# Expert phase of a two-layer hybrid backbone: pairs of experts in units of 64 slots, half of the sums kept in PSUM

## The chip, the core and the metric

One core of a Trainium2 chip runs the whole program. The metric is device time in microseconds (us), the median of several executions. Engines: PE (TensorE, matmuls), DVE (VectorE), ACT (ScalarE), POOL (GpSimd), and SP, which here only starts transfers. Each engine runs its own instruction list in order and waits for others by semaphores.

## The reference

Two layers over 512 tokens of width 1024. Each layer has a mixer (attention and convolution in layer 0, a gated MLP in layer 1) and then a mixture of experts, the part that the change touches:

```python
def hier_moe(h, ...):                       # 512 tokens, D 1024
    gidx = argmax(group logits)             # one of 4 groups, weight gw
    tv, ti = lax.top_k(expert logits of that group, 2)
    ew = softmax(tv) * gw                   # 2 of 32 experts for a token
    for e in range(32):                     # D_EXPERT 256
        he = (silu(t @ w_gate[e]) * (t @ w_up[e])) @ w_down[e]
        out = out + dense_w[:, e:e + 1] * he
x = x + g2 * hier_moe(h2)
```

512 tokens with two experts each are 1024 slots, 32 for an expert on the mean, but the router decides how many each expert gets.

## The kernel before

The 32 experts are taken as 16 pairs (e, e + 16), and for each pair SP streams six tiles of 1 MB. Tokens are first sorted by expert into four tiles `xs`, so that an expert's tokens are a run of columns. A pair unit takes 64 slots of each of both experts:

- gates and up, `gate_up` (L357): 16 matmuls of 512 columns, the two experts in the two halves of the array's columns, into bank `pg`;
- `act` (L362 on ACT, L363 on DVE) and `turn` (L370 transposes, L371 copy) give the hidden activations, transposed;
- `down` (L430): 8 matmuls into two banks `py`;
- `weigh` (L419 on DVE, L420 on ACT, L421 on DVE): multiplies by the token's weight and by g2 and splits the product in a rounded high part and a rest, so that the scatter can use the faster fp32r matmuls;
- `add_half` (L400): a matmul with a one-hot matrix (L388, L389) brings each of the four token tiles and two column halves back to token order, once for the high part and once for the rest, and DVE (L413) or ACT and POOL (L410, L411) add the half to X.

If an expert of the pair has more than 64 tokens, `again` runs a unit for the next 64 of that expert (L451 gates, L459 down) in another part of PSUM. That is decided at run time by `tc.If`. Both arms of the If (L623) hold the gates of the next pair (`first(j + 1, ...)`), with the scatter of this pair behind them in PE's list; a hint on PE (L480, L482) names the likely arm ahead of time. The order of everything is that of the Python code; there is no scheduler.

In PE's list a pair is thus: `down` of j, branch, gates of j + 1, scatter of j in two parts around the transposes of j + 1, `down` of j + 1. DVE's weighing of j has the time of the gates of j + 1. Weight tiles for the next pairs are asked for at the end of each pair (`st.emit(6, j)`, issued at L322 and L324).

Of the kernel before, what the change touches and what calls it, by code (L numbers as in the profile page):

```python
# [8 lines left out]
F32 = mybir.dt.float32  # L9
# [8 lines left out]
P = 128  # L18
# [3 lines left out]
SLOT = 64  # L22

# [93 lines left out]
class Route:  # L117
# [37 lines left out]
    def end(self, res):  # L155
# [23 lines left out]
        R0 = k.work.tile([P, 8, 64], BF16, name="R0", tag="w2", bufs=NW2)  # L179
# [22 lines left out]
        with nc.allow_low_precision(reason="whole numbers under 512"):  # L202
            v.tensor_reduce(res.g0, p0[:, 0:2], axis=AX.X, op=OP.add)
# [10 lines left out]
        pin(v.tensor_copy(it[:, 0], ro[:, 0]))  # L214
# [8 lines left out]
    def starts(self, res):  # L223

        k, cc = self.k, self.cc
        v = k.nc.vector
        cm = k.small.tile([P, 16], F32, name="cm", tag="cm")
        for r in range(8):
            v.tensor_scalar(res.start[:, r], cc[:, 32:64], float(SLOT * r), 1024.0 - SLOT, op0=OP.add, op1=OP.min)
        v.tensor_tensor(cm, cc[:, 0:16], cc[:, 16:32], op=OP.max)  # L230
        v.tensor_copy(res.cnt[:, 0, :], cm)
        res.most = k.work.tile([P, 1], I32, name="most", tag="most")
        v.tensor_reduce(res.most, cm, axis=AX.X, op=OP.max)
        v.tensor_scalar(cc[:, 0:32], cc[:, 0:32], float(SLOT), None, op0=OP.is_gt)
        v.scalar_tensor_tensor(res.cnt[:, 2, :], cc[:, 16:32], 2.0, cc[:, 0:16], op0=OP.mult, op1=OP.add)
        v.tensor_scalar(cc[:, 0:16], cm, 2.0 * SLOT, None, op0=OP.is_gt)
        v.scalar_tensor_tensor(res.cnt[:, 3, :], res.cnt[:, 2, :], 3.0, cc[:, 0:16], op0=OP.is_equal, op1=OP.max)
        v.tensor_scalar(cm, cm, float(SLOT - 1), None, op0=OP.add)
        v.tensor_copy(res.cnt[:, 1, :], cm)
        v.tensor_scalar(res.cnt[:, 1, :], res.cnt[:, 1, :], 6, None, op0=OP.arith_shift_right)  # L240

        d = k.small.tile([P, 2, 16], F32, name="d", tag="rd")
        v.tensor_scalar(d[:, 0], res.cnt[:, 2, :], 2.0, None, op0=OP.is_equal)
        v.tensor_tensor(d[:, 1], res.start[:, 1, 16:32], res.start[:, 1, 0:16], op=OP.subtract)
        v.tensor_tensor(d[:, 1], d[:, 1], d[:, 0], op=OP.mult)
        v.tensor_tensor(res.second, d[:, 1], res.start[:, 1, 0:16], op=OP.add)
# [27 lines left out]
    def columns(self, r):  # L274
# [8 lines left out]
        for c, C in enumerate(self.C):  # L283
# [3 lines left out]
            v.tensor_tensor(C[:, :, 0], C[:, :, 0], b(k.tok1[:, s]), op=OP.mult)  # L287

# [45 lines left out]
def moe_bufs(k):  # L334
# [15 lines left out]
    return m  # L350


def gate_up(k, m, st, p, cs):

    for c in cs:
        for h in range(2):
            k.nc.tensor.matmul(m.pg[64 * h:64 * h + 64, :], m.xT[:, c, 64 * h:64 * h + 64], st.gu(p, h, c), start=(c == 0), stop=(c == 7))  # L357


def act(k, m):  # L360

    k.nc.scalar.activation(m.sg, m.pg[:, 0:256], AF.Silu)  # L362
    k.nc.vector.tensor_tensor(m.h, m.sg, m.pg[:, 256:512], op=OP.mult)  # L363


def turn(k, m, n=P):

    nc = k.nc
    for f in range(2):
        nc.tensor.transpose(m.ph[:, f * P:f * P + n], m.h[0:n, f * P:(f + 1) * P], k.ident[0:n, 0:n])  # L370
    nc.scalar.copy(m.hT[:, :, 0:n], m.ph[:, 0:2 * P].rearrange("p (f s) -> p f s", f=2)[:, :, 0:n])  # L371


SIDE = [(0, 1), (2, 0)]
SIDE0 = ()


class Outs:
# [3 lines left out]
    def __init__(self, oh, y):  # L382
        self.oh, self.y = oh, y
        self.left = ()

    def where(self, k, m, tok):
        eng = k.nc.vector
        eng.tensor_scalar(m.t4, k.noff, tok, None, op0=OP.add)  # L388
        eng.tensor_tensor(self.oh.rearrange("p (i t) -> p i t", i=NT), k.iota[:, None, :].to_broadcast([P, NT, P]),  # L389
                                m.t4[:, :, None].to_broadcast([P, NT, P]), op=OP.is_equal)  # L390

    def add(self, k, m, X, tiles):

        for i in tiles:
            for n in range(2):
                self.add_half(k, m, X, i, n)

    def sum_half(self, k, po, i, n, start=True, stop=True):
# [4 lines left out]
    def add_half(self, k, m, X, i, n, side=SIDE):  # L403
        c = slice(512 * n, 512 * n + 512)
        po = m.po[(2 * i + n) % 4]
        if (i, n) in self.left:
            m.one.sum_half(k, po, i, n, stop=False)
# [1346 lines left out]
```

## Time and profile before

| | us |
|---|---|
| median of 3 runs | 1422.37 (1417.93 to 1423.74) |
| the profiled execution | 1433.02 |
| its span | 1431.2 |
| PE busy | 1288.0 (90%) |
| DVE busy | 850.7 (59%) |
| ACT busy | 558.8 (39%) |
| POOL busy | 319.0 (22%) |
| mean granted clock of PE | 0.951 |

The two expert phases lie at about 445 to 723 us (layer 0) and 1091 to 1431 us (layer 1). Times in rows count from the start of the span. In a timeline row stand the start, the length from the first to the last of the grouped instructions, engine, line, operation, out<-in, shape and count, and in brackets how long the engine sat idle before and what ended that. One fp32 matmul instruction of the code is two records of the trace: x32 at L357 are the 16 matmuls of a pair.

### The profile page before, as it was taken

The page shows a single profiled execution, that of the slowest core. Times are in us where ns is not written, and L with a number is a line of the kernel's source. Part 1 is how long each engine was busy: PE and PEld are TensorE (multiplying, and loading weights), DVE is VectorE, ACT ScalarE, POOL GpSimd, SP SyncE. Part 2 cuts the span into 40 slices and gives each one's busy share as a digit, 9 for nine tenths or more (in the row PEclk, how much of TensorE's full clock was granted, in tenths as well). Part 3 has the DMA queues.
Part 4 walks back from the last instruction along what each step waited for, and adds up shares of the span by engine and source line. Part 5 has one row for each costly group of instructions (what it writes and reads, how often), then busy time and mean ns, then how long its engine had stood idle before and what let it go on. Part 6 is the DMA issues. An engine that isn't in the chain of part 4 may idle for free. (4 is left out here: it accounts for less than half of the span.)

```text
span 1431.2 us, 20527 instructions
## 1 busy us (share of the span) xinstructions
PE 1288.0 (90%) x7174; PEld 835.3 (58%) x7174; DVE 850.7 (59%) x1730; ACT 558.8 (39%) x1315; POOL 319.0 (22%) x289
## 2 busy tenths in 40 slices
PE   5999878899996989989969999999995999999997
PEld 3678754454774444444458898997873444444443
DVE  2334687889667546564684455676347566555554
ACT  3244544476444424333352233344324433332331
POOL 0033454587102112121230001220002022111210
PEclk9999988899997999999989999999997999999998
DMA  9411044726546789989856354353367687877771
GB/s 360 156 32 44 17 167 135 293 72 221 221 166 248 287 345 412 413 348 387 354 181 224 123 203 159 133 196 133 122 253 272 261 359 310 344 293 291 297 306 61
DMA packets 54570, 329.12 MB, mean 230 GB/s; under 512 B 8030, under 2 KB 8286, under 8 KB 19634
## 3 DMA queue, kind: packets, MB, share of 16 engines
q1 hardware_dynamic: 48658, 306.29, 55.3%
q0 software_dynamic: 5664, 19.93, 4.3%
q8 instruction: 106, 1.74, 0.5%
q14 instruction: 142, 1.16, 0.2%
HBM read 317.77 MB, written 8.43 MB: 228 GB/s over the span
## 5 line engine op out<-in xcount | busy, mean ns | idle before, releaser
L357 PE MATMUL mps<-w,xT 128*64 128x512 f32 x1024 | 245.2, 632 | 27.6 <-PEq L480 10.1
L357 PEld LDWEIGHTS mps<-w,xT 128*64 128x64 f32 x1024 | 90.3, 145 | 175.9 <-issue 171.0
L411 POOL TENSOR_TENSOR X<-X,tmp 128x512 f32<-128x512 f32 x72 | 92.9, 1291 | 443.1 <-ACT tmp L410 386.4
L700 PE MATMUL ps_c<-wch,hxh 128*128 128x256 f32 x512 | 147.6, 288 | 2.0 <-ACT hxh L706 2.0
L702 PE MATMUL ps_c<-wch,hxl 128*128 128x256 f32 x512 | 145.8, 285 | 1.5 <-DVE rm_m L98 0.9
L701 PE MATMUL ps_c<-wcl,hxh 128*128 128x256 f32 x512 | 146.0, 286 | 0.0
L400 PE MATMUL mps<-oy,ooh 128*128 128x512 f32 x512 | 138.8, 408 | 1.7 <-ACTq L623 1.7
L413 DVE TENSOR_TENSOR X<-X,mps 128x512 f32<-128x512 f32 x206 | 132.8, 683 | 10.8 <-PE mps L400 9.0
L363 DVE TENSOR_TENSOR mix<-mix,mps 128x256 f32<-128x256 f32 x32 | 13.5, 421 | 185.6 <-ACT mix L362 185.6
L430 PE MATMUL mps<-w,mix 128*64 128x512 f32 x512 | 116.9, 598 | 0.0
L400 PEld LDWEIGHTS mps<-oy,ooh 128*128 128x128 f32 x512 | 91.4, 189 | 43.0 <-issue 22.2
L891 POOL TENSOR_TENSOR acc<-acc,ctp 128x497 f32<-128x497 f32 (+14 forms) x71 | 101.8, 1462 | 32.9 <-ACT ctp L890 32.9
L700 PEld LDWEIGHTS ps_c<-wch,hxh 128*128 128x128 f32 x512 | 98.9, 193 | 7.8 <-issue 4.2
L701 PEld LDWEIGHTS ps_c<-wcl,hxh 128*128 128x128 f32 x512 | 99.0, 193 | 4.2 <-issue 3.4
L702 PEld LDWEIGHTS ps_c<-wch,hxl 128*128 128x128 f32 x512 | 98.8, 193 | 4.5 <-issue 1.7
L362 ACT ACTIVATE mix<-mps 128x256 f32<-128x256 f32 x32 | 12.3, 384 | 202.5 <-PE mps L357 199.7
L430 PEld LDWEIGHTS mps<-w,mix 128*64 128x64 f32 x512 | 33.9, 136 | 66.1 <-issue 55.2
L700 PE MATMUL ps_o<-woh,yTh 128*128 128x512 f32 x160 | 64.7, 406 | 2.1 <-ACT v L1333 1.2
L420 ACT CAST oy<-mps 128x512 fp32r<-128x512 f32 x64 | 37.2, 585 | 75.0 <-DVE mps L419 75.0
L706 POOL TENSOR_TENSOR vs<-v,vs 128x512 fp32r<-128x512 f32 x16 | 23.0, 1440 | 182.1 <-ACT vs L706 174.7
L701 PE MATMUL ps_o<-wol,yTh 128*128 128x512 f32 x160 | 63.3, 396 | 0.0
L702 PE MATMUL ps_o<-woh,yTl 128*128 128x512 f32 x160 | 62.9, 394 | 0.0
(412 smaller groups left out, 2527.7 us busy)
## 6 DMA issues: line engine op xcount, KB each, us to landing
w<-in_w_gu_dram SPq DMA_DIRECT2D x128, 1024.0 KB
w<-in_w_down_dram SPq DMA_DIRECT2D x64, 1024.0 KB
wada<-in_w_ada_dram SPq DMA_DIRECT2D x48, 1024.0 KB
wc<-in_c_w_in_dram SPq DMA_DIRECT2D x16, 1024.0 KB
wo<-in_c_w_out_dram SPq DMA_DIRECT2D x8, 1024.0 KB
X<-in_x_dram SPq DMA_DIRECT2D x4, 1024.0 KB
wo<-in_ab_w_out_dram SPq DMA_DIRECT2D x4, 1024.0 KB
h2d<-row POOLq DMA_DIRECT2D x16, 256.0 KB, 5.2
```

The lines of the kernel that those rows point to most:

```text
L357: k.nc.tensor.matmul(m.pg[64 * h:64 * h + 64, :], m.xT[:, c, 64 * h:64 * h + 64], st.gu(p, h, c), start=(c == 0), stop=(c == 7))
L363: k.nc.vector.tensor_tensor(m.h, m.sg, m.pg[:, 256:512], op=OP.mult)
L400: k.nc.tensor.matmul(po, self.oh[:, i * P:i * P + P], y[:, 512 * n:512 * n + 512], start=start and y is self.y[0], stop=stop and y is self ...
L411: k.nc.gpsimd.tensor_tensor(X[i][:, c], X[i][:, c], m.tmp, op=OP.add)
L413: k.nc.vector.tensor_tensor(X[i][:, c], X[i][:, c], po, op=OP.add)
L420: nc.scalar.copy(hi, py[s])
L430: nc.tensor.matmul(m.py[n][64 * h:64 * h + 64, :], m.hT[:, f, 64 * h:64 * h + 64], st.dn(p, h, f)[:, 512 * n:512 * n + 512], start=(f == 0 ...
L700: k.nc.tensor.matmul(out, lh, rh, start=start, stop=False)
L701: k.nc.tensor.matmul(out, lh, rl, start=False, stop=False)
L702: k.nc.tensor.matmul(out, ll, rh, start=False, stop=stop)
L706: for i in (k.nc.scalar.copy(hi, src), (eng or k.nc.vector).tensor_tensor(lo, src, hi.bitcast(F32), op=OP.subtract)):
L891: nc.gpsimd.tensor_tensor(d, d, tp, op=OP.add)
```

## The change

- A head unit holds the first 32 tokens of both experts of a pair. Its 64 rows stand in `xT` (now 64 wide), and its gates and up go to four column tiles of 32: gate of the first expert, gate of the second, up of the first, up of the second, 256 columns each. `down` does the same with the two halves of the output, and the result of a unit is one bank `py` instead of two.
- Tokens from the 33rd on are done by expert, 64 slots in a unit, in two column tiles (gate and up), inside `tc.If(n > HEAD)`, one If for each expert. Inside it a second If (`n > HEAD + SLOT`) holds a loop for tokens beyond the 96th.
- All units, heads and others, use the same banks: `pg`, `ph` (halves of bank 0), `py` (bank 1), two banks `po`, and four banks `acc`.
- The high part and the rest of a unit stand in one tile `y`, in the two halves of the partitions, so that one matmul sums both: 8 scatter matmuls a unit. The four for the first half of the columns add up in `acc` for the whole phase and are added to X at its end (`final`); the four for the second half go through `po` and are added to X by DVE in each unit.
- ACT and POOL add nothing to X any more, and the branch hints are gone. The next gates stand behind the Ifs and not in their arms.
- A unit's scatter is issued in the next unit, behind its gates, and the last two adds behind the weighing of the unit that issues it (`run`).
- The one-hot matrix comes from one comparison of a row of token numbers (`seq`) with the token of each slot. The row and the two halves of g2 are loaded by three POOL transfers. The banks `acc` are cleared by four matmuls with zeros.
- Further rounds of columns (`later`, four passes) are computed where an expert has more than 96 tokens; before, three passes where one had more than 128.

The diff, cut to the parts that make and run a unit; the functions removed are those shown above (`gate_up`, `act`, `turn`, `Outs`, `weigh`, `down`, `weighed`, `again`, `first`, `second`, `others`).

```diff
-    m.pg, m.ph, m.py, m.po = ps[0], ps[1], ps[2:4], ps[4:8]
-    m.xT = k.work.tile([P, 8, P], F32, name="xT", tag="xT")
+    m.pg, m.ph, m.py, m.po, m.acc = ps[0][:, 0:256], ps[0][:, 256:512], ps[1], ps[2:4], ps[4:8]
+    m.last = m.po + [ps[1], ps[0]]
+    m.xT = k.work.tile([P, 8, SLOT], F32, name="xT", tag="xT")
+    m.xr = [k.work.tile([P, 8, SLOT], F32, name="xr", tag=f"xr{h}") for h in range(2)]
...
+class Unit:
+    def __init__(self, k, m, st, p, h=None):
+        self.k, self.m, self.st, self.p = k, m, st, p
+        if h is None:
+            self.parts = [(slice(HEAD * q, HEAD * q + HEAD), slice(HEAD * (q % 2), HEAD * (q % 2) + HEAD), q % 2, q // 2) for q in range(4)]
+            self.x = m.xT
+        else:
+            self.parts = [(s, A, h, q) for q, s in enumerate((A, B))]
+            self.x = m.xr[h]
+    def gates(self, cs=range(8)):
+        for c in cs:
+            for r, s, h, q in self.parts:
+                self.k.nc.tensor.matmul(self.m.pg[r], self.x[:, c, s], self.st.gu(self.p, h, c)[:, 256 * q:256 * q + 256], start=(c == 0), stop=(c == 7))
+    def act(self):
...
+        nc.scalar.activation(m.sg[A], m.pg[A], AF.Silu)
+        nc.vector.tensor_tensor(m.h[A], m.sg[A], m.pg[B], op=OP.mult)
...
+    def weigh(self, w, tok):
+        v, m = self.k.nc.vector, self.m
+        y, c = m.y, [slice(0, 512), slice(512, D)]
+        v.scalar_tensor_tensor(m.py, m.py, w, m.g2h, op0=OP.mult, op1=OP.mult)
+        for s, cs in zip((A, B), c):
+            self.k.nc.scalar.copy(y[s, cs], m.py[s])
+        v.tensor_scalar(m.oh, m.seq, tok, None, op0=OP.is_equal)
+        for s, o, cs in zip((A, B), (B, A), c):
+            v.tensor_tensor(y[o, cs], m.py[s], y[s, cs].bitcast(F32), op=OP.subtract)
+
+def scatter(k, m, ps, i, n, start, stop):
+    k.nc.tensor.matmul(ps, m.oh[:, i * P:i * P + P], m.y[:, 512 * n:512 * n + 512], start=start, stop=stop)
...
-    with tc.If(nc.values_load(res.most[0:1], min_val=0, max_val=512, skip_runtime_bounds_check_because="counts of at most 512 tokens") > 2 * SLOT):
-        for r in (2, 4, 6):
+    with tc.If(nc.values_load(res.most[0:1], min_val=0, max_val=512, skip_runtime_bounds_check_because="counts of at most 512 tokens") > SLOT + HEAD):
+        rt.later(res)
+        for r in (2, 4, 6, 8):
             rt.columns(r)
...
+    for ps in m.acc:
+        nc.tensor.matmul(ps, m.oh[:, 0:P], m.oh, start=True, stop=False)
+
+    def run(u, w, tok, turned=None):
+        u.gates()
+        u.act()
+        for i in range(4):
+            scatter(k, m, m.acc[i], i, 0, False, False)
+        u.turn()
+        for i in range(2):
+            scatter(k, m, m.po[i], i, 1, True, True)
+            add(m.po[i], i, 1)
+        if turned:
+            turned()
+        u.down()
+        for i in range(2):
+            scatter(k, m, m.po[i], i + 2, 1, True, True)
+        u.weigh(w, tok)
+        for i in range(2):
+            add(m.po[i], i + 2, 1)
+
     for j in range(16):
         p = pair(j)
...
+        seconds(j)
+        w, tok = res.tw0[:, 1, p:p + 1], res.tw0[:, 0, p:p + 1]
         if j:
-            down(k, m, st, p)
+            run(Unit(k, m, st, p), w, tok, (lambda: heads(j + 1)) if j < 15 else None)
+        else:
+            u.weigh(w, tok)
+        for h in range(2):
+            e = p + 16 * h
+            u = Unit(k, m, st, p, h)
+            n = value(0, e, 512)
+            with tc.If(n > HEAD):
+                run(u, res.tw[:, 1, 1, e:e + 1], res.tw[:, 1, 0, e:e + 1])
+                with tc.If(n > HEAD + SLOT):
+                    with tc.For_i(2, value(1, e, 9), 1) as r:
...
+                        run(u, m.tw[:, h, 1:2], m.tw[:, h, 0:1])
         st.emit(6, j)
```

PE's list before, in the arm of a pair without further units: gates of the next pair (L357, bank `mps_3747`), then the scatter (L400). "waits" names the semaphores that an instruction waits for: `DVE_49` is VectorE's count, `Activation_49` ScalarE's, `DMAHW` a weight transfer.

```order
L357 MATMUL mps_3747<-w,xT 64x512 [waits DMAHW2_49,Activation_49]
L357 MATMUL mps_3747<-w,xT 64x512 [waits DMAHW3_49,Activation_49]
L357 MATMUL mps_3747<-w,xT 64x512 x3
L357 MATMUL mps_3747<-w,xT 64x512 [waits Activation_49]
L357 MATMUL mps_3747<-w,xT 64x512 x2
L357 MATMUL mps_3747<-w,xT 64x512 [waits DMAHW4_49]
L357 MATMUL mps_3747<-w,xT 64x512 [waits DMAHW5_49,Activation_49]
L357 MATMUL mps_3747<-w,xT 64x512 x3
L357 MATMUL mps_3747<-w,xT 64x512 [waits Activation_49]
L357 MATMUL mps_3747<-w,xT 64x512 x2
L400 MATMUL mps_3751<-oy_4103,ooh 128x512 [waits DVE_49,Activation_49]
L400 MATMUL mps_3751<-oy_4104,ooh 128x512 [waits DVE_49]
```

The gates wait for weights and for ScalarE; VectorE is waited for from the first scatter matmul on.

PE's list after, from the end of the second expert's If (lines 563 and 561 of the changed kernel) into the next head: gates at its line 378, bank `mps_3744`, scatter at line 413.

```order
L563 UNCONDITIONAL_BRANCH [waits PE_49,PE_sequencer_49]
L561 UNCONDITIONAL_BRANCH [waits PE_49,PE_sequencer_49]
L378 MATMUL mps_3744<-w,xT 32x256 [waits DMAHW2_49,DVE_49,Activation_49]
L378 MATMUL mps_3744<-w,xT 32x256 [waits DMAHW3_49]
L378 MATMUL mps_3744<-w,xT 32x256 x14
L378 MATMUL mps_3744<-w,xT 32x256 [waits DMAHW4_49]
L378 MATMUL mps_3744<-w,xT 32x256 [waits DMAHW5_49]
L378 MATMUL mps_3744<-w,xT 32x256 x14
L413 MATMUL mps_3748<-y,oh 128x512 [waits DVE_49,Activation_49]
L413 MATMUL mps_3749<-y,oh 128x512
L413 MATMUL mps_3750<-y,oh 128x512
L413 MATMUL mps_3751<-y,oh 128x512
```

The two branches are the not-taken paths of the Ifs, where an engine waits for its own count before it raises it; the first gate matmul behind them waits for VectorE's count. That count includes what VectorE's not-taken path adds.

PE's list after, from the end of a head unit into the first expert's further unit.

```order
L413 MATMUL mps_3746<-y,oh 128x512 [waits DVE_49]
L413 MATMUL mps_3747<-y,oh 128x512 [waits DVE_49]
L420 TENSOR_LOAD cnt
L561 COMPARE_AND_BRANCH
L378 MATMUL mps_3744<-w,xr 64x256 x16
L413 MATMUL mps_3748<-y,oh 128x512 [waits DVE_49,Activation_49]
L413 MATMUL mps_3749<-y,oh 128x512
```

Here the gates (L378) stand in the If's arm directly behind the branch and wait for nothing; only the scatter waits for VectorE.

DVE's list before, from the end of the Ifs to the next branch: the one-hot (L388, L389), the multiply by the weight (L419) and the subtraction (L421) of a pair.

```order
L623 UNCONDITIONAL_BRANCH [waits DVE_sequencer_49]
L388 TENSOR_SCALAR t_3765<-ct,tok_102 128x4 [waits DVE_49]
L389 TENSOR_TENSOR ooh<-ct,t_3765 128x512 [waits DVE_49]
L419 SCALAR_TENSOR_TENSOR mps_3749<-mps_3749,w_103,g_3759 128x512 [waits PE_49]
L419 SCALAR_TENSOR_TENSOR mps_3750<-mps_3750,w_103,g_3759 128x512 [waits PE_49]
L421 TENSOR_TENSOR oy_4104<-mps_3749,oy_4103 128x512 [waits Activation_49]
L421 TENSOR_TENSOR oy_4104<-mps_3750,oy_4103 128x512 [waits Activation_49]
L473 TENSOR_LOAD cnt
L623 COMPARE_AND_BRANCH
```

The list goes from the last subtraction straight to the branch; the adds of that pair (L413) stand in the arms.

DVE's list after, from the end of an If through a head unit to its branch: the multiplication of `act` (line 384), adds to X (528), the multiply by the weight (403), the one-hot (406), the subtractions (408).

```order
L561 UNCONDITIONAL_BRANCH [waits DVE_49,DVE_sequencer_49]
L384 TENSOR_TENSOR mix<-mix,mps_3744 64x256 [waits Activation_49]
L528 TENSOR_TENSOR X_3073<-X_3073,mps_3746 128x512 [waits DVE_49,PE_49]
L528 TENSOR_TENSOR X_3073<-X_3073,mps_3747 128x512 [waits DVE_49,PE_49]
L403 SCALAR_TENSOR_TENSOR mps_3745<-mps_3745,tw_101,g_3758 128x512 [waits DVE_49,PE_49]
L406 TENSOR_SCALAR oh<-g_3758,tw_101 128x512 [waits PE_49]
L408 TENSOR_TENSOR y<-mps_3745,y 64x512 [waits DVE_49,Activation_49]
L408 TENSOR_TENSOR y<-mps_3745,y 64x512
L528 TENSOR_TENSOR X_3074<-X_3074,mps_3746 128x512
L528 TENSOR_TENSOR X_3074<-X_3074,mps_3747 128x512
L420 TENSOR_LOAD cnt
L561 COMPARE_AND_BRANCH
```

Two of the four adds of the unit before now stand behind the weighing, ahead of the load and the branch of line 561.

## Rows read from the trace of the kernel before

**Rows 1.** The page: each engine's busy time, share of the span, instructions.
```profile
PE 1288.0 (90%) x7174; PEld 835.3 (58%) x7174; DVE 850.7 (59%) x1730; ACT 558.8 (39%) x1315; POOL 319.0 (22%) x289
```

**Rows 2.** One window of layer 0's pairs without overflow, by engine.
```profile
core 0: us, PE busy (x) PEld busy (x) DVE busy (x) ACT busy (x) POOL busy (x), PEclk, DMA share, GB/s
540.00:612.00 72.00, 72.00 (x328) 31.98 (x326) 42.79 (x65) 26.53 (x88) 12.42 (x10) 1.00 1.01 412
```

**Rows 3.** Timeline of PE, one pair: start, length, operation, count.
```profile
556.71 7.04 PE L357 MATMUL mps<-w,xT 128*64 128x512 f32 x32
...
567.82 3.65 PE L430 MATMUL mps<-w,mix 128*64 128x512 f32 x16
...
571.30 7.04 PE L357 MATMUL mps<-w,xT 128*64 128x512 f32 x32
```

**Rows 4.** Timeline of all engines around the overflow unit of layer 0.
```profile
615.08 3.62 PE L451 MATMUL mps<-w,mix 128*64 128x256 f32 x32
...
619.22 0.42 DVE L453 TENSOR_TENSOR mix<-mix,mps 64x256 f32<-64x256 f32 x1 [1.82 <-ACT mix L452]
...
620.23 0.33 PE L370 MATMUL mps<-ct,mix 64*128 64x64 f32 x2
...
620.61 0.27 ACT L371 COPY mix<-mps 128x128 f32<-128x128 f32 x1
...
621.63 1.94 PE L459 MATMUL mps<-w,mix 128*64 128x512 f32 x8
...
623.62 0.75 DVE L419 SCALAR_TENSOR_TENSOR mps<-mps,rw,g 64x512 f32<-64x512 f32 x1 [0.79 <-PE mps L459]
...
624.79 7.09 PE L357 MATMUL mps<-w,xT 128*64 128x512 f32 x32 [1.22 <-PEq L480]
...
625.01 0.77 DVE L419 SCALAR_TENSOR_TENSOR mps<-mps,rw,g 64x512 f32<-64x512 f32 x1 [0.65 <-ACT oS L420]
...
626.43 1.39 DVE L421 TENSOR_TENSOR oS<-mps,oS 64x512 fp32r<-64x512 f32 x2 [0.65 <-ACTq L639]
```

**Rows 5.** Groups of instructions: busy, mean ns, idle before and its end.
```profile
L413 DVE TENSOR_TENSOR X<-X,mps 128x512 f32<-128x512 f32 x206 | 132.8, 683 | 10.8 <-PE mps L400 9.0 <-DVEq L623 0.7
...
L451 PE MATMUL mps<-w,mix 128*64 128x256 f32 x224 | 25.4, 379 | 1.8 <-ACT oy L420 1.8
...
L389 DVE TENSOR_TENSOR ooh<-ct,t 128x512 fp32r<-128x512 f32 x32 | 22.1, 692 | 1.1
```

**Rows 6.** Timeline of PE: a product in four 32-wide column tiles.
```profile
203.99 1.07 PE L720 MATMUL ps_ada<-wada,sc 128*32 128x512 f32 x8
```

**Rows 7.** Timeline of layer 0's first round of columns.
```profile
456.56 0.42 DVE L285 TENSOR_TENSOR C<-ct,ft 128x256 f32<-128x256 f32 x1
...
462.47 1.95 PE L292 MATMUL mps<-C,S 128*128 128x128 f32 x16
```

**Rows 8.** Timeline of PE where it starts after a gap.
```profile
474.66 8.88 PE L357 MATMUL mps<-w,xT 128*64 128x512 f32 x32 [2.43 <-ACT xT L490]
...
509.87 10.04 PE L357 MATMUL mps<-w,xT 128*64 128x512 f32 x32 [4.03 <-issue]
...
718.49 4.46 PE L400 MATMUL mps<-oy,ooh 128*128 128x512 f32 x16 [1.67 <-ACTq L623]
...
1120.31 8.61 PE L357 MATMUL mps<-w,xT 128*64 128x512 f32 x32 [2.40 <-ACT xT L490]
...
1316.93 8.95 PE L357 MATMUL mps<-w,xT 128*64 128x512 f32 x32 [2.20 <-ACT oy L420]
...
1362.78 7.18 PE L357 MATMUL mps<-w,xT 128*64 128x512 f32 x32 [2.06 <-ACT oy L420]
```

**Rows 9.** Window behind the longest of these gaps, columns as before.
```profile
509.87:513.00 3.13, 3.13 (x8) 1.46 (x10) 0.00 (x0) 0.00 (x0) 0.00 (x0) 0.50 0.22 42
```

**Rows 10.** PE's branches of line 623: duration ns least, median, most.
```profile
L623 PEldq COMPARE_BRANCH  x39: 82/363/6427, 473.4 to 1403.6; - x39
```

**Rows 11.** Timeline of DVE at the program's end.
```profile
1422.50 4.87 DVE L676 TENSOR_TENSOR X<-X,mps 128x512 f32<-128x512 f32 x8 [0.16 <-PE mps L400]
```

More of the change, by code (lines that the diff above doesn't have):

```diff
@@ L346, in moe_bufs @@
     m.xs = [W(k, [P, 2, D], "xs") for _ in range(4)]
     m.ic = k.small.tile([P, 2], I32, name="ic", tag="ic")
-    m.t4 = k.small.tile([P, NT], F32, name="t4", tag="t4")
     m.tw = k.small.tile([P, 2, 2], F32, name="tw", tag="tw")
+    m.t1 = k.small.tile([P, 1], F32, name="t1", tag="t1")
     return m
[L353 to L357, printed above, removed]
@@ L360, in act @@
[L360 to L398, printed above, removed]
-        for y in self.y:
-            k.nc.tensor.matmul(po, self.oh[:, i * P:i * P + P], y[:, 512 * n:512 * n + 512],
-                               start=start and y is self.y[0], stop=stop and y is self.y[-1])
[L403 to L407, printed above, removed]
-        self.sum_half(k, po, i, n, (i, n) not in self.left)
-        if (i, n) in side:
-            k.nc.scalar.copy(m.tmp, po)
-            k.nc.gpsimd.tensor_tensor(X[i][:, c], X[i][:, c], m.tmp, op=OP.add)
-            return
-        k.nc.vector.tensor_tensor(X[i][:, c], X[i][:, c], po, op=OP.add)
@@ L484, in window, with value @@
-    def window(x, at, act=False):
+    def value(row, e, most, **kw):
+        return nc.values_load(res.cnt[0:1, row, e:e + 1], min_val=0, max_val=most,
+                              skip_runtime_bounds_check_because="counts of at most 512 tokens", **kw)
+    def window(x, at, n=SLOT, act=True):
         e = mybir.EngineType
-        o = nc.values_load(at, engines=(e.Activation if act else e.DVE,), min_val=0, max_val=1024 - SLOT,
-                           skip_runtime_bounds_check_because="starts of at most 960")
+        o = nc.values_load(at, engines=(e.Activation if act else e.DVE,), min_val=0, max_val=1024 - n,
+                           skip_runtime_bounds_check_because="starts of at most 960, or of 992 for 32")
@@ L570, in experts @@
-    m.one = Outs(tile([P, 512], "oh"), [tile([P, D], f"y{i}") for i in range(2)])
-    m.two = Outs(tile([P, 512], "C0"), [tile([P, D], "S")])
-    m.tmp = k.work.tile([P, 512], F32, name="tmp", tag="C1")
-    def first(j, due):
-        ahead_of(f"few{l}_{j}", 0, pair(j), 512, SLOT)
-        gate_up(k, m, st, pair(j), range(8))
-        act(k, m)
-        due.add(k, m, X, (0, 1))
-        turn(k, m)
-        if j < 15:
-            windows(j + 1)
-        due.add(k, m, X, (2, 3))
-    ends = [(n, i) for n in range(2) for i in range(4)]
+                u.down()
+            else:
+                heads(1)
@@ L680, in experts, with final @@
             ahead()
-    if l == 0:
-        nc.scalar.activation(m.t4[:, 0:1], k.eps6, AF.Sqrt)
-        done(lambda i, n: m.one.add_half(k, m, X, i, n, SIDE0))
+    def final(i, n):
+        if n == 0:
+            scatter(k, m, m.acc[i], i, 0, False, True)
+            add(m.acc[i], i, 0)
+        else:
+            scatter(k, m, m.last[i], i, 1, True, True)
+            add(m.last[i], i, 1)
+    if l == 0:
+        nc.scalar.activation(m.t1, k.eps6, AF.Sqrt)
+        done(final)
+    else:
+        for n in range(2):
+            for i in range(4):
+                final(i, n)
+                done(i, n)
 def W(k, shape, name, dt=F32):
@@ L1468 @@
 ROWAHEAD = 0
-FILL = [[(0, 0), (0, 1), (1, 0)], [(1, 1), (2, 0)]]
-LEFT = [(i, n) for i in range(4) for n in range(2) if (i, n) not in FILL[0] + FILL[1]]
 COLWAIT = 3
```

281 lines of the change are left out of this document (88 added, 193 removed).

## The prediction

> **What bounds the kernel now.** I read the page's engine shares first: TensorE (PE) is busy 90% of 1431.2 us and VectorE (DVE) 59% [rows 1]. Then, because that share is an average, a window over undisturbed pairs of layer 0's expert phase: PE 72 of 72 us, DVE 42.79 of 72, granted clock 1.00, and the DMA engines full at 412 GB/s [rows 2]. Then the PE timeline of one pair: gate/up matmuls 7.04 us, then the transposes and scatter matmuls, down 3.65 us, and the next pair's gates start as the down ends, so a pair takes 571.30 − 556.71 = 14.59 us [rows 3]. PE is the bound there and weight streaming stands beside it. VectorE's weighing of pair j (about 4 us) costs nothing only because PE computes the gates of pair j+1 meanwhile. That cover is what I follow below.
>
> How many units the changed kernel runs depends on tokens per expert, which I worked out from the reference's router on its inputs. Layer 0: 14 experts above 32 tokens, 1 above 64, none above 96. Layer 1: 11, 6 and 2 (both 103). The trace agrees where it can: 224 records at L451 are 7 units of 32 [rows 5].
>
> **The change part by part.**
>
> *Matmul work.* A head unit's gates are 64 records of 256 columns in four column tiles, where the pair had 32 of 512 in two. No such gates are in the trace. The nearest row is eight four-tile records of 512 columns in 1.07 us, so two rounds of four, 0.5 us each [rows 6]; 64 records of 256 are then 16 rounds of about 0.25, 4.0 us or less. From the other side, 32 records of 256 columns in two tiles, also 16 rounds, took 3.62 [rows 4]. I take 3.5. A further unit's gates are that 3.62 itself; its down is the 1.94 of L459 [rows 4], the head's the same. Scatter falls from 16 to 8 matmuls a unit. By matmuls alone a unit is about 7.5 us, and there are 16 + 14 = 30 in layer 0, 16 + 11 + 2 = 29 in layer 1.
>
> *The cover.* Before, the next gates stand inside each arm, and the few that follow the end of an If write a bank that the further unit did not use: at 624.79 they start while DVE still has an L419 at 625.01 and the L421 at 626.43 to do [rows 4]. After, all units write the same bank, each If is closed before the next gates, and those gates wait for DVE's count, which the not-taken path of the If raises on DVE only when DVE's own work is done (the order rows of PE and DVE). So the next gates wait for the weighing and also for the two adds behind it. Only a first-expert unit straight behind its head is spared.
>
> *Price of a serialized unit, at full clock.* Gates to the end of the multiplication: 615.08 to 619.22 + 0.42 = 4.56. Transposes to the copied hT: 620.23 to 620.88 = 0.65, with 0.2 for handing over 0.85. Down 1.94 [rows 4]. Then on DVE one after the other: the weighing multiply 0.75 [rows 4], the one-hot comparison 0.69 (nearest row: the comparison of 128x512 at L389), two adds of 0.683 [rows 5], two subtractions in 1.39 [rows 4], which is 4.19; hand-overs and branch 0.25. Sum 11.8 us, in which PE idles about 4.4 behind its down. A head followed by a first-expert unit costs only 4.56 + 0.85 + 1.94 + 0.15 = 7.5. Two Ifs' branches on DVE I put at 0.6 a pair; nothing shows it exactly, the compare-branches of PE run from 0.08 to 6.43 us [rows 10], and up to 4 us of a slow one hide behind DVE's tail.
>
> A pair with neither expert above 32 thus takes 12.4, with the first only 19.9, the second only 24.2, both 31.7. Layer 0 has 4, 5, 5 and 2 of these: 333.5 us. The tail of pair 0 starts near 472 (474.66 less the gap of 2.43 before it [rows 8]), 7.4 us into its unit, so the last unit ends at 472 + 326 = 798. Before, the closing scatter starts at 718.49 [rows 8]: +80. Layer 1 has 6, 3, 6 and 1: 311 us, plus two loop passes at 15 (a unit, four copies and the loop's hand-overs; no row has one, I allow 12 to 20). It also runs the four extra rounds of columns, since 103 is above 96: six VectorE operations of 0.42 and 1.95 us of matmuls each, partly beside each other [rows 7], about 3.7 with the copies, 15 in all; before, its limit of 128 was not passed. Layer 1's tail of pair 0 starts near 1118 (1120.31 less 2.40 [rows 8]); from there 1118 + 15 + 341 − 7.4 = 1467, and the eight closing adds with their stores take about 8.7, as now (from 1422.50 [rows 11] to the span's end): 1476, +45. The DMA queue stops being near its limit, as pairs now take 20 us or more where 14.59 kept it full.
>
> *Removed.* ACT's and POOL's share of the adds, the zeroing and the prefetch hints were beside PE's work [rows 2] and give nothing back. One-hot and g2 loads by POOL in the prologue I price at 0 (hidden by the 2.43 us gap before the first gates [rows 8]) to 3 us.
>
> *The clock.* A gap of 2.06 us left the 32 gate records at 7.18, one of 2.20 made them 8.95, and one of 4.03 made them 10.04 instead of 7.04; after that one the granted clock was 0.50, the 1.2 GHz level, from 509.87 to 513 [rows 8, 9]. After the change PE idles about 4.4 us before 22 units of layer 0 and 24 of layer 1, which is nearest to the last of these rows: 3.0 us each, 46 × 3.0 = 138. Bounds: 0, if the clock holds as after 2.06, and 5.1, if gates, down and scatters of each unit run at 1.2 GHz from end to end (3.4 + 1.7 more), 235 in all.
>
> The Trainium skill, "TensorE: Matmul & The Clock Gate", section "What's actually happening", says that for modelling the ramp costs under 1% of a typical kernel's span; by that the clock would add under 14 us (an estimate from that page) and the time would be near 1560, the first rival below. The trace speaks against it here, with 3.0 us after a single gap [rows 8], and the change makes 46 of them. The page "TensorEngine Tiling (Array Packing)" of the Trainium skill, section "PSUM Bottleneck", warns that column tiling speeds the matmuls but not the reading of PSUM behind them. The rows agree: DVE's 4.19 us a unit does not shrink with half the slots.
>
> *Sum.* +80 + 45 + 138 = +263 on the profiled execution's 1433.0 us (span 1431.2 with 1.8 around it): 1696. The median of the runs shown is 1422.4, 10.7 below that execution; the same +263 gives 1685. Some gaps may fall short of the full 3.0, as the rows near 2 us differ among themselves; I say 1680.
>
> **The rivals.**
>
> *The clock holds* (or costs little): +125 alone, 1547. For it: gates after 2.06 us kept full speed. Against: the row at 4.03.
>
> *The cover survives: faster.* Its place is the wait in front of the gates behind an If, and it decides by whether DVE's count is there when PE has issued its down. If so, a unit is PE's 3.5 + 8 scatters of 0.25 + 0.33 + 1.94 = 7.8, and layer 0 is 30 × 7.8 = 234, against 16 × 14.59 = 233 of streaming: no change. Layer 1 would be 27 × 7.8 + 30 + 15 = 256 from 1120 where 302 pass now [rows 8], about −40. Total near 1385. For it: at 624.79 gates did start beside DVE's tail behind an If. Against: those do not wait for DVE in the order, and these do.
>
> *PE stays at 1.2 GHz and unhinted jumps stall it:* 46 × 5.1 = 235 instead of 138, and compare-branches like the slowest (6.43, 2 more than the tail covers [rows 10]) at a third of 64 Ifs, +40: about 1780 to 1820. For it: PE would be busy barely 60% of a unit. Against: of 39 branches at L623 the median is 0.36 [rows 10], and the gates behind the 4.03 gap lost 3.0 us of a possible 7 [rows 8]. The Trainium skill, "Runtime: NRT & Kernel Launch", section "Instruction fetch mechanics", says that a taken branch beyond the fetched pages waits for a fetch; the 6.43 agrees, the median does not.
>
> *The change does not do what it says* (layer counts other than I worked out): a few units more or less, 15 us each; inside the range.
>
> **How the numbers follow.** Forecast, serialized with a clock loss of 1.5 to 4 us each (1615 to 1730): 0.55. Clock holds or costs under 1.5 (1540 to 1615): 0.22. Slow clock and stalls above 1730: 0.13. Cover survives: 0.10, of which 0.07 faster, and 0.03 where fixed extras eat the gain. The range leaves out the cover's 0.10 and most of what lies above 1745: 1540 to 1745. A measurement of this kernel tells about 0.5% (7 us) from no change; faster 0.07, same 0.02, slower 0.91.
>
> **What would show it.** PE's rows should read gates of 3.5 (or up to 7 at 1.2 GHz), each behind a gap of about 4.4 us put down to DVE's add of X, 46 times; a layer-0 window with PE near 60%, DVE near half and the DMA share well under 1.00; PEclk well below 1.00 there; first-expert gates without a gap. Layer 0's phase should grow by some 120 us or more, layer 1's by some 90 to 120. Gates that follow the down without a gap would make the whole forecast wrong; gaps with gates still at 3.5 us would leave 1547.

## The result and the profile after

The changed kernel takes 1700.3 us (median of 4 runs, 1697.0 to 1705.23) against 1421.05 us of the kernel before in the same runs: 1.197 times the time before, 95% interval 1.193 to 1.201. Forecast were 1680 us. The profiled execution has a span of 1697.5 us against 1431.2, so 266.3 us are to be found.

First the engines of the changed kernel, as in [rows 1], and the two groups of its gate matmuls (heads read `xT`, further units `xr`). Behind the second bar stands how long PE was idle just before them, and what ended most of it.

```profile
PE 1333.1 (79%) x9142; PEld 888.2 (52%) x9142; DVE 875.4 (52%) x1805; ACT 574.1 (34%) x1451; POOL 231.2 (14%) x221
...
L378 PE MATMUL mps<-w,xT 128*32 128x256 f32 x2048 | 181.0, 524 | 158.4 <-DVEq L561 85.8
...
L378 PE MATMUL mps<-w,xr 128*64 128x256 f32 x864 | 129.2, 465 | 70.3 <-DVEq L561 47.5
```

PE went from 90% to 79% of a longer span, and no engine took its place as the one that is always busy. The two groups alone hold 228.7 us of idle PE, and L561 is the If on an expert's count. The answer to [rows 2] is a window of layer 0's pairs, with one of layer 1's:

```profile
core 0: us, PE busy (x) PEld busy (x) DVE busy (x) ACT busy (x) POOL busy (x), PEclk, DMA share, GB/s
480.00:600.00 120.00, 85.47 (x650) 43.22 (x650) 51.64 (x85) 32.96 (x118) 0.00 (x0) 0.85 0.62 245
1300.00:1600.00 300.00, 209.64 (x1484) 106.05 (x1488) 114.95 (x199) 71.91 (x258) 0.00 (x0) 0.84 0.59 233
```

PE is busy 71% and 70%, the granted clock fell from 1.00 to 0.85, and the weights stream at 245 GB/s instead of 412: the queue that stood full waits too. The PE timeline of pairs 1 to 3 answers to [rows 3]:

```profile
483.56 4.92 PE L378 MATMUL mps<-w,xT 128*32 128x256 f32 x64 [4.24 <-DVEq L563]
488.41 1.20 PE L413 MATMUL mps<-y,oh 128*128 128x512 f32 x4
489.54 0.34 PE L390 MATMUL mps<-ct,mix 64*128 64x64 f32 x2
489.80 0.73 PE L413 MATMUL mps<-y,oh 128*128 128x512 f32 x2
490.46 1.92 PE L397 MATMUL mps<-w,mix 128*32 128x512 f32 x16
492.31 0.73 PE L413 MATMUL mps<-y,oh 128*128 128x512 f32 x2
492.98 3.67 PE L378 MATMUL mps<-w,xr 128*64 128x256 f32 x32
...
506.82 5.29 PE L378 MATMUL mps<-w,xT 128*32 128x256 f32 x64 [5.57 <-DVEq L561]
...
521.02 4.98 PE L378 MATMUL mps<-w,xr 128*64 128x256 f32 x32 [4.33 <-DVEq L561]
...
534.83 6.57 PE L378 MATMUL mps<-w,xT 128*32 128x256 f32 x64 [4.25 <-DVEq L563]
```

Both forms of unit stand here. The first-expert unit at 492.98 follows its head without a gap, and its gates take 3.67 us. All other gates in these rows stand behind 4.24 us or more, and take 4.92 to 6.57. The granted clock of two of them, columns as in the window above:

```profile
492.98:496.65 3.67, 3.67 (x34) 2.27 (x33) 2.76 (x6) 1.16 (x2) 0.00 (x0) 1.00 0.00 0
521.02:526.00 4.98, 4.98 (x33) 3.19 (x33) 0.00 (x0) 0.00 (x0) 0.00 (x0) 0.73 0.00 0
```

1.00 is the 2.4 GHz level; 0.73 is a mean of the two levels. No weights were moving in either stretch, so the slow gates are not a matter of transfers here. On DVE the gap in front of 521.02 is this:

```profile
518.82 0.69 DVE L408 TENSOR_TENSOR y<-mps,y 64x512 fp32r<-64x512 f32 x1
519.53 1.28 DVE L528 TENSOR_TENSOR X<-X,mps 128x512 f32<-128x512 f32 x2
520.99 0.33 PEld L378 LDWEIGHTS mps<-w,xr 128*64 128x64 f32 x4 [4.73 <-issue]
521.02 4.98 PE L378 MATMUL mps<-w,xr 128*64 128x256 f32 x32 [4.33 <-DVEq L561]
```

The weighing and its two adds end at 520.81, and 0.2 us later PE starts. PE itself is ready sooner: in its records its last branch ends 0.81 us into this gap of 4.33, and in all 42 gaps that have no loop beside them it ends at least 0.29 us before the gates start. Layer 0's closing scatter, at 718.49 before [rows 8], is now at 858.22, behind 5.60 us of idle PE: +140. The rest, about +125, is layer 1's. There stand the four rounds of columns and a loop pass:

```profile
1260.21 3.33 PE L295 MATMUL mps<-C,S 128*128 128x128 f32 x16 [3.51 <-DVE C L283]
...
1276.61 3.19 PE L295 MATMUL mps<-C,S 128*128 128x128 f32 x16 [1.84 <-DVE C L283]
...
1356.54 5.35 PE L378 MATMUL mps<-w,xr 128*64 128x256 f32 x32 [4.95 <-DVE xr L429]
...
1371.15 6.54 PE L378 MATMUL mps<-w,xT 128*32 128x256 f32 x64 [4.68 <-DVE X L528]
```

The rounds last from 1258.02 to 1279.84, 22 us. The loop's unit lasts 1371.15 − 1356.54 = 14.6 us.

### The profile page after: what moved, and what is told of

It is laid out like the page before. It is cut to its first block, busy times and chain, and to the rows that moved or that the text cites. A ratio compares the mean times of both kernels' runs of the same rounds, so it can differ in the third digit from the quotient of the medians.

```text
span 1697.5 us, 25793 instructions
## 1 busy us (share of the span) xinstructions
PE 1333.1 (79%) x9142; PEld 888.2 (52%) x9142; DVE 875.4 (52%) x1805; ACT 574.1 (34%) x1451; POOL 231.2 (14%) x221
## 5 line engine op out<-in xcount | busy, mean ns | idle before, releaser
L378 PE MATMUL mps<-w,xT 128*32 128x256 f32 x2048 | 181.0, 524 | 158.4 <-DVEq L561 85.8
L378 PEld LDWEIGHTS mps<-w,xT 128*32 128x32 f32 x2048 | 100.6, 149 | 236.1 <-issue 138.5
L378 PE MATMUL mps<-w,xr 128*64 128x256 f32 x864 | 129.2, 465 | 70.3 <-DVEq L561 47.5
L413 PE MATMUL mps<-y,oh 128*128 128x512 f32 x472 | 159.0, 441 | 9.9 <-DVEq L561 5.6
L378 PEld LDWEIGHTS mps<-w,xr 128*64 128x64 f32 x864 | 80.2, 169 | 118.0 <-issue 85.1
L413 PEld LDWEIGHTS mps<-y,oh 128*128 128x128 f32 x472 | 77.2, 192 | 90.7 <-DVE X L528 47.1
L405 ACT CAST y<-mps 64x512 fp32r<-64x512 f32 x118 | 68.4, 580 | 151.6 <-DVE mps L403 150.2
L397 PE MATMUL mps<-w,mix 128*32 128x512 f32 (+1 forms) x728 | 113.9, 600 | 0.0
L408 DVE TENSOR_TENSOR y<-mps,y 64x512 fp32r<-64x512 f32 x118 | 81.3, 689 | 52.8 <-ACTq L563 19.9
L429 ACT COPY xr<-xs 128x128 f32 x256 | 58.0, 295 | 95.0 <-DVEq L561 44.3
```

Of the source, the lines that this page charges most:

```text
L378: self.k.nc.tensor.matmul(self.m.pg[r], self.x[:, c, s], self.st.gu(self.p, h, c)[:, 256 * q:256 * q + 256], start=(c == 0), stop=(c == 7))
L397: self.k.nc.tensor.matmul(self.m.py[r], self.m.hT[:, f, s], self.st.dn(self.p, h, f)[:, 512 * q:512 * q + 512], start=(f == 0), stop=(f == 1))
L405: self.k.nc.scalar.copy(y[s, cs], m.py[s])
L408: v.tensor_tensor(y[o, cs], m.py[s], y[s, cs].bitcast(F32), op=OP.subtract)
L413: k.nc.tensor.matmul(ps, m.oh[:, i * P:i * P + P], m.y[:, 512 * n:512 * n + 512], start=start, stop=stop)
L429: (nc.scalar.copy if act else nc.vector.tensor_copy)(x[:, 2 * c:2 * c + 2], m.xs[c][:, :, bass.ds(o, n)])
```

## The experiments

Every kernel starts from the changed one; `+` and `-` are against it, if nothing else is said. The kernel before ran beside them with a median of 1422 to 1429 us.

**late_adds: two adds less in the tail.** The last two adds of a unit are issued in the next one, behind its gates.

```diff
         u.gates()
+        for i in range(2):
+            add(m.po[i], i + 2, 1)
         u.act()
...
         u.weigh(w, tok)
-        for i in range(2):
-            add(m.po[i], i + 2, 1)
```

> The two adds behind each unit's weighing are moved behind the branch, to the start of the next unit on DVE (the two po banks are cleared once at the start, and two adds close the phase). My theory, that gates behind an If wait for the end of DVE's own work: the gap before those gates shrinks from 4.24-4.33 to about 2.9 us, 46 x 1.37 = 63 us less, and up to 40 more if gaps of 2.9 lose less clock than gaps of 4.3: 1595 to 1640. Rival, that the gap is PE's own sequencer (loads, branches, fetches) or ACT: unchanged, 1700 within 7.

It takes 1632.92 us, 67 less. Of PE's timeline:

```profile
503.67 6.53 PE L378 MATMUL mps<-w,xT 128*32 128x256 f32 x64 [4.28 <-DVEq L563]
...
517.80 3.67 PE L378 MATMUL mps<-w,xr 128*64 128x256 f32 x32 [3.02 <-DVEq L563]
```

These are the units at 506.82 and 521.02 of the changed kernel, where the gaps were 5.57 and 4.33. The ordinary gap is 2.9 to 3.0 us instead of 4.3, less by the 1.28 us of the two adds: what stands last on DVE does set the start of the gates. A shorter gap does not always leave the clock whole: heads' gates in layer 0 have a mean of 5.76 us (waits for weights inside them included; 5.58 in the changed kernel), further units' 4.02 (4.48).

**warm: the clock by itself.** Ten matmuls with zeros run in front of the gates behind an If, so that PE has worked just before them. (The first expert's unit behind its head has none.)

```diff
+        for _ in range(warm):
+            nc.tensor.matmul(m.acc[0][:, 0:P], m.zero, k.ident, start=False, stop=False)
         u.gates()
```

> Ten matmuls that add zeros to an accumulating bank (2 records each, about 2.7 us) stand on PE in front of the gates of every unit but the first expert's. They wait for nothing. If the slow gates (4.9 to 6.6 us instead of 3.67) come from the clock that fell in the gap: gates back at 3.7 to 4, 46 x 1.97 = up to 90 us less, 1610 to 1640, gaps plus filler as long as before. If the gates are slow for another reason (weights arriving, four column tiles, semaphores): 1700 or some us more.

It takes 1703.17 us, no less, where up to 90 us less were expected. Of its timeline, its windows and its waits:

```profile
504.29 4.40 PE L535 MATMUL mps<-ct,zero 128*128 128x128 f32 x20 [7.61 <-PEq L565]
508.62 3.66 PE L378 MATMUL mps<-w,xT 128*32 128x256 f32 x64
```

```profile
504.29:508.62 4.33, 4.33 (x20) 4.21 (x21) 0.00 (x0) 0.83 (x4) 0.00 (x0) 0.53 0.93 325
508.62:512.28 3.66, 3.66 (x66) 2.05 (x65) 0.00 (x0) 0.00 (x0) 0.00 (x0) 1.00 1.00 410
```

```profile
PE mps L535 <- PEq L565: 84.3, 17, 8.4
```

The zeros run at a granted clock of 0.53 and the gates behind them at 1.00, and these are back at 3.66. Added up over the units the gates take 223.7 us, and 305.4 in the changed kernel, so the slow clock takes 82 us there. But the zeros start only when PE is through its own branch, and run 2.4 to 7.0 us. Gap and zeros together grew by as much as the gates won.

**warm_end: the same at the other end.** Six such matmuls at the end of each unit, ahead of the weighing and the branch.

```diff
         for i in range(2):
             scatter(k, m, m.po[i], i + 2, 1, True, True)
+        for _ in range(6):
+            nc.tensor.matmul(m.acc[0][:, 0:P], m.zero, k.ident, start=False, stop=False)
         u.weigh(w, tok)
```

> As warm, but six matmuls that add zeros (12 records, 1.6 us) stand at the end of every unit, ahead of the branch, so that they run while DVE weighs and PE's branch is not later than DVE's count. If half a gap is short enough for the clock: gates at 3.7 to 4.3 in most of 46 places, up to 82 us less, 18 us more where a first-expert unit follows directly: 1635 to 1660. If the branch stands behind the filler and ends the gap later, or 2.7 us of idling lose as much clock as 4.3: 1700 or above.

It takes 1738.23 us, 38 more: the worse of the two outcomes that the expectation named.

```profile
522.22 5.29 PE L378 MATMUL mps<-w,xr 128*64 128x256 f32 x32 [2.98 <-DVEq L565]
```

The zeros fill the first part of the gap, 2.98 us are left, and behind those the gates are as slow as before (heads in layer 0: 6.34 us in the mean, waits for weights inside them included). The filler is paid and buys nothing.

**no_ifs: no branch, more work.** All three units of every pair run.

```diff
-            n = value(0, e, 512)
-            with tc.If(n > HEAD):
-                run(u, res.tw[:, 1, 1, e:e + 1], res.tw[:, 1, 0, e:e + 1])
-                with tc.If(n > HEAD + SLOT):
...
+            run(u, res.tw[:, 1, 1, e:e + 1], res.tw[:, 1, 0, e:e + 1])
```

> No Ifs in the expert phase: head, first and second expert's further unit of every pair run one behind the other, whether they hold tokens or not: 48 units a layer instead of 30 and 29 (tokens beyond an expert's 96th, in layer 1, are left out). Theory, that a unit itself is cheap and only the Ifs' ends are dear: no gap before any gates, granted clock near 1.00, 8.2 us a unit as a head in front of a first-expert unit shows now, 47 x 8.24 = 387 us a layer: layer 0 within 15 us of the changed kernel's, total 1680 to 1720 with 60% more units. Rival, that the small units (column tiles of 32, 256 columns, eight scatters) are themselves slow: 13 us each as now on the mean, 47 x 13 = 611 a layer, total above 2100.

It takes 1679.58 us, with 48 units a layer instead of 30 and 29. The window is that of above:

```profile
480.00:600.00 120.00, 120.00 (x929) 59.16 (x926) 80.75 (x133) 41.28 (x138) 0.00 (x0) 1.00 0.67 256
```

```profile
502.07 3.67 PE L378 MATMUL mps<-w,xr 128*64 128x256 f32 x32
510.27 3.66 PE L378 MATMUL mps<-w,xT 128*32 128x256 f32 x64
518.45 3.67 PE L378 MATMUL mps<-w,xr 128*64 128x256 f32 x32
```

PE never stops, its clock is whole, and a unit takes 8.19 us though all units still share their banks. So neither the shared banks nor VectorE's work by itself cost the time: what does is that a program part ends between a unit and the next gates. The rows give the floor of the design too. From the first further unit's gates of layer 0 on there are 29 units; at 8.19, and with the 5.60 us ahead of the closing scatter, that is 243 us. The kernel before needed 243.8 (474.66 to 718.49, [rows 8]). Only the start of that stretch is sooner in the changed kernel, 469.69, so there were some 5 us to win in that layer even with every other wait gone.

**one_bank and own_bank: a bank of their own for the heads' gates.** To have a bank free, the scatters that are added at once share one (`po`), and are spread over the unit; the last is added behind the weighing. One_bank is that alone, with `m.gate[0]` for both kinds of unit; own_bank, below, has the heads' gates and transposes in bank 0 and the further units' in bank 1.

```diff
-    m.pg, m.ph, m.py, m.po, m.acc = ps[0][:, 0:256], ps[0][:, 256:512], ps[1], ps[2:4], ps[4:8]
+    m.gate, m.py, m.po, m.acc = ps[0:2], ps[2], ps[3:4], ps[4:8]
...
         if h is None:
-            self.x = m.xT
+            self.x, g = m.xT, m.gate[0]
         else:
-            self.x = m.xr[h]
+            self.x, g = m.xr[h], m.gate[1]
```

> Control for own_bank: the four second-half scatters go through a single po bank, one before the accumulating ones, one behind them, one in the middle of down and one behind it, so that only one add stays behind the weighing; the loop's windows are copied by ACT. All units still share one gate bank. Theory: gap 3.6 instead of 4.3, 46 x 0.68 = 31 us less and a little clock: 1650 to 1670. Rival (the order of scatters costs PE more than the add it saves): 1700 or above.

> As one_bank, but the heads' gates and transposes have a bank of their own, which nothing inside the Ifs touches; further units keep the other. Theory: the gates of 30 heads (15 in each layer) no longer wait for DVE and start as the down before them ends; 30 x (3.6 gap + 1.5 to 2 of clock) = 155 to 170 us less than one_bank: about 1490 to 1510. The 14 second-expert units and 2 loop passes still wait. Rival 1, that the gap is PE's branches and not the bank: as one_bank. Rival 2, that another wait (ACT's copies of the token windows, the shared activation tile) takes its place: half of the gain or less.

One_bank takes 1717.33 us, as its rival had it: the ordinary gaps shrink to 3.9, but from the end of its gates on a unit is some 0.5 us longer on PE, as the scatters wait for the one bank. Own_bank takes 1646.4, 71 less than its control, less than half of what was expected. Three heads of it:

```profile
526.77 3.57 PE L379 MATMUL mps<-w,xT 128*32 128x256 f32 x60 [0.69 <-PEq L570]
...
547.94 5.25 PE L379 MATMUL mps<-w,xT 128*32 128x256 f32 x64 [3.47 <-ACT xr L430]
...
564.64 4.26 PE L379 MATMUL mps<-w,xT 128*32 128x256 f32 x41 [6.41 <-DMA w<-in_w_gu_dram]
```

The first starts 0.69 us behind PE's work, as the prediction's rival "the cover survives" wanted it; so do 11 of the 30 heads, at 0.7 to 0.8 us. At the others something else is late once VectorE isn't: PE's own way through the Ifs (19.0 us in four places by the view of waits), ScalarE's copies (38.9 in ten), a weight transfer.

**own_hint: own_bank with branch hints on PE** for both Ifs, set in the unit before.

```diff
+    def ahead_of(e):
+        c = value(0, e, 512, engines=(mybir.EngineType.PE,))
+        tc.mark_branch_hint_location(f"few{l}_{e}", hint=c > HEAD, engines=(mybir.EngineType.PE,))
...
-            with tc.If(n > HEAD):
+            few = tc.If(n > HEAD, preferred_fallthrough_block=True, label=f"few{l}_{e}")
+            with few as other:
```

> As own_bank, with a prefetch hint on PE for each of the two Ifs (for the first behind the head's gates, for the second behind the first-expert unit's gates or in the not-taken arm). Theory, that in own_bank PE's own jumps took the place of the wait for DVE: the heads' gaps of 1.7 to 6.9 us shrink to about 0.8, 83 us to 30 or 40 in all, and the clock holds before 15 to 20 more heads, 30 us: 1646 to about 1570. Rival, that what is left are weights not yet there or ACT's copies: gaps as in own_bank, 1630 to 1650.

It takes 1654.5 us, no less than own_bank's 1646.4. Of its waits:

```profile
PE mps L379 <- PEq L576: 60.2, 12, 6.8
```

With these hints PE's own way through the Ifs ends more of the gaps, 60.2 us in twelve places where it was 19.0 in four. So the run shows that these hints do not help, and leaves open whether late code is what holds PE there.

**no_deep: the inner If out.** Only the If for an expert's first further unit stays.

```diff
             with tc.If(n > HEAD):
                 run(u, res.tw[:, 1, 1, e:e + 1], res.tw[:, 1, 0, e:e + 1])
-                with tc.If(n > HEAD + SLOT):
-                    with tc.For_i(2, value(1, e, 9), 1) as r:
...
-                        run(u, m.tw[:, h, 1:2], m.tw[:, h, 0:1])
```

> The inner If and its loop are taken out (tokens beyond an expert's 96th are left out; the extra rounds of columns stay). Two loop passes go, with the barrier behind a loop: 2 x 17 = 34 us. If the gaps above 4.3 us (5.2 to 10.5, 30 us in all) come from jumps over the long arms, which are half as long now: up to 22 more, 1640 to 1650. If they do not: about 1666, gaps of 5.3 to 8 remain.

It takes 1539.02 us, 161 less, where 34 to 56 were expected. Two heads of its PE timeline:

```profile
500.10 5.35 PE L378 MATMUL mps<-w,xT 128*32 128x256 f32 x64 [4.26 <-DVEq L561]
...
524.00 3.66 PE L378 MATMUL mps<-w,xT 128*32 128x256 f32 x64
```

The head at 524.00 follows a further unit that was run, without a gap and at full clock; the one at 500.10 follows an If that was not taken. VectorE's list at the end of an If says why. First the changed kernel (the way past the inner If's arm and the way past the outer's), then no_deep (the end of the arm, and the way past it):

```
L563 UNCONDITIONAL_BRANCH [waits DVE_49,DVE_sequencer_49]
L561 UNCONDITIONAL_BRANCH [waits DVE_49,DVE_sequencer_49]
```

```
L561 UNCONDITIONAL_BRANCH
L561 UNCONDITIONAL_BRANCH [waits DVE_49]
```

An arm that was run ends without a wait; the way past an arm waits for the engine's own work before it raises the count to what the arm would have made it. In the changed kernel every arm that is run ends in the inner If's way past (in layer 1 two end in the loop), so the wait comes in both cases. Of the 161 us some 30 are the two loop passes that no_deep leaves out (14.6 us each, above); about 130 are the inner If's, which was never taken in layer 0. Beside the loop the expectation had only the longer gaps in view. They are gone too: what the gaps hold above 4.3 us each falls from 30 us to 5. But 46 gaps have also become 28.

**no_deep_late and no_deep_own: the three together.** The first is no_deep with late_adds' edit, the second no_deep with own_bank's and its one late add moved likewise.

> As no_deep (the inner branch and its loop are gone, tokens beyond the 96th of an expert are left out), and as in late_adds the two last additions of a unit are issued behind the branch, at the start of the next unit. No_deep took 1539.0 us with some 28 gaps of 4.3 to 5.3 us ahead of the gates, each behind an If that isn't taken. If such a gap is the drain of VectorE's tail, late_adds' 1.3 us a gap (67 us over 46 gaps) is taken off 28 of them: 1495 to 1510 us. If the gap there is the jump and the weights instead, the additions are beside it and the time stays at 1530 to 1540 us.

> As no_deep (tokens beyond the 96th of an expert are left out), with the heads' gates in a PSUM bank of their own, one bank for the scatters that are added at once, and the unit's last addition issued at the start of the next unit. If what is left in no_deep is the wait of a head's gates for VectorE's drained work behind an If that isn't taken (28 gaps of about 5 us and 2 us each of slower gates, 196 us), two thirds or more of it goes: 1400 to 1450 us, near the kernel before. If a jump of TensorE or VectorE or a transfer of weights stands right behind that wait, as in own_bank (46% of what was expected there), 1470 to 1500 us.

They take 1497.74 and 1474.15 us. The first is as the drain of VectorE has it; the second misses 1450 and lies in the second range of its expectation. Of the waits of no_deep_own:

```profile
PE mps L379 <- DVEq L569: 36.4, 11, 4.0
...
PE mps L379 <- PEq L569: 13.2, 14, 1.4
```

Its heads hardly wait now; what is left are eleven further units, of about 3.3 us each, behind a first expert's If that wasn't taken. In layer 0 its closing scatter is at 763.73, 45 us behind the 718.49 of before, as a unit with the one bank `po` takes 8.82 us.

Idle PE in front of the gates, added up from the PE rows over both layers (layer 0's first head, ahead of all the Ifs, is left out), and the time of the gates from the first to the last of a group, in us. In own_bank 17 us of that time are idle inside the groups; in the others it is at most 4.

| kernel | median us | idle before heads | before further units | gates |
|---|---|---|---|---|
| changed | 1700.3 | 157.9 | 70.3 | 305.4 |
| late_adds | 1632.9 | 124.4 | 51.7 | 289.1 |
| one_bank | 1717.3 | 141.0 | 64.6 | 312.3 |
| own_bank | 1646.4 | 82.9 | 64.4 | 308.5 |
| no_deep | 1539.0 | 77.8 | 47.5 | 261.1 |
| no_deep_late | 1497.7 | 56.6 | 34.0 | 247.7 |
| no_deep_own | 1474.2 | 16.6 | 37.1 | 236.2 |

Between the changed kernel and no_deep, idle time and gates fall by 103 + 44 us; most of the rest of the 161 is what is left of the loop's units. None of the versions reaches the kernel before, and the floor of layer 0 says why none with these units can beat it by much. Layer 1 needed 302 us before, from the gates of its second pair on; the 28 units from there at 8.19, 13 us more for two loop passes, 22 for the rounds of columns and 4 of idle time ahead of the closing scatter are 268. An estimate from these rows is therefore that some 40 us, 3%, were the most that the change could have brought.

## Why the prediction was right, and where its sizes were off

*The mechanism: right.* The gates wait behind 46 Ifs' ends, 22 in layer 0 and 24 in layer 1, as counted from the router, and the ordinary gap, 25 of the 46, is 4.23 to 4.33 us where 4.4 stood. No_ifs takes the wait away and PE is busy throughout; late_adds takes 1.28 us of VectorE's tail away and the gap falls by as much. "Only a first-expert unit straight behind its head is spared" is the row at 492.98. What the prediction didn't see is that a run arm waits only because of the inner If: it put the wait on the If in general, and no_deep shows that nearly half of the price, about 130 of 279 us, hung on an If that is hardly ever taken.

*Layer 0 with its clock +146, layer 1 +117 (sums of the forecast's terms): measured +140 and about +125.* Inside them errors cancel, so that 1680 stands as near to 1700.3 as it does is in part luck:

- A unit straight behind its head was put at 7.5 us, and is 8.19. The sum went from the gates to the down and left out the two scatters behind it (0.73 at 492.31). The same two are missing from the 11.8 of a serialized unit, 4.25 + 8.19 = 12.4; 59 units are some 39 us too little.
- Head gates were put at 3.5 and take 3.66 at full clock; the one-hot at 0.69 by its nearest row, and takes 0.48.
- The four rounds of columns: 15 forecast, 22 measured. PE was idle between them, and the row of 1.95 us [rows 7] became 3.2 to 3.8.
- The clock was put at 3.0 us a gap, 138 in all. By warm it is 82, some 1.8 a gap (against 3.67 a group the gates of the changed kernel are 91 us longer, and warm leaves 9 of these). The step that failed is the choice of the row at 4.03 [rows 8] as the nearest: there the granted clock was 0.50 for 3.13 us [rows 9], while here gates behind 4.24 take anything from 4.92 to 6.57 instead of 3.67.
- Four gaps are longer, 7.6 to 10.5 us; all that is above 4.3 a gap adds up to 30 us. For the branches the forecast held 0.6 a pair, 19 in all, and more only in its slow rival. Here is a longer gap, with VectorE's last work ahead of it:

```profile
556.98 1.29 DVE L528 TENSOR_TENSOR X<-X,mps 128x512 f32<-128x512 f32 x2
...
562.17 0.90 ACT L429 COPY xr<-xs 128x128 f32 x4 [2.86 <-DVEq L561]
562.18 1.08 PE L378 MATMUL mps<-w,xT 128*32 128x256 f32 x8 [8.01 <-DVEq L561]
```

VectorE is done at 558.27 and both wait for its sequencer until 562.17. Its records put 559.09 to 562.06 between one branch and its next step.

With these, +263 − 47 (clock, 91 instead of 138) + 39 + 7 + 11 (30 above the ordinary gap, less the 19) − 6 (the tail of pair 0 starts at 465.5, not near 472) is +267, against 266 measured.

*The rivals.* "The clock holds" is out by the gates' rows, though it is nearer than 138 us made it look: with nothing but the gates' clock restored the kernel would be at about 1620 (an estimate, 1700 less 82). The figure of the Trainium skill that stood beside it ("TensorE: Matmul & The Clock Gate", "What's actually happening": under 1% for the ramp of a typical kernel) doesn't fit this kernel, which pays once a gap: 82 of 1700 us are 4.8%. "The cover survives" happened in own_bank for some heads, at 0.69 us, by a bank of its own, which is how the prediction explained the cover of the kernel before. "Slow clock and stalls" has its stalls in the longer gaps, 30 us where it put 40, and not its clock.

## What to carry to other kernels

An If costs on the way that is *not* taken: each engine then waits for its own work before it hands its count on, so an If at the end of an arm puts that wait behind every arm that is run, though it is hardly ever taken itself. Before work is moved from an arm to behind an If, ask which banks and buffers it shares with what the engines still do at the If's end, and count how often the program passes there. A tail of VectorE that costs nothing beside the next matmuls costs PE more than its length when it stands alone: here 4.3 us of gap brought 1.8 us of slower matmuls with them on the mean.

## What the runs showed of the hardware

- Work straight in front of the gates gives most of them their clock back (3.66 us at a granted clock of 1.00 behind the zeros at 504.29 in warm; 3.71 is the mean of layer 0's heads there, 5.58 in the changed kernel). Behind gaps near 3 us both full and slow gates occur: 3.67 us, clock 1.00, behind 3.02 in late_adds, and 5.29 us, clock 0.69, behind 2.98 in warm_end.
- A jump of VectorE held PE for some 3 us (559.09 to 562.06), where the prediction had priced two branches of VectorE at 0.6. The Trainium skill, "Runtime: NRT & Kernel Launch", "Instruction fetch mechanics", has a taken branch beyond the fetched pages wait for a fetch. A wait of that kind is in these records, but no run here shows that a fetch made it: hints were tried on PE alone, and brought nothing (1654.5 against 1646.4).
- Gates in four column tiles with 64 records of 256 columns take 3.66 us, in two tiles with 32 records 3.67: twice the instructions at the same time.
